# Splitting every weight of the first layer's front part, with the rests computed on GpSimd

## The chip, the cores and the metric

The kernel runs on one core of one Trainium2 chip, in one launch. The metric is the device time of the whole program in microseconds (us), and lower is better. A core has TensorE (PE, with its weight loads as PEld), VectorE (DVE), ScalarE (ACT), GpSimd (POOL) and SyncE (SP), which here issues all the transfers, and 16 DMA engines that carry them out.

## The reference

The reference is a decoder trunk with two layers over 256 tokens of 2048 channels, all in float32. Cut to what matters here:

```python
c_act = silu(c)
for l in range(2):
    mod = c_act @ w_mod[l] + b_mod[l]                  # w_mod[l]: 2048 x 12288
    shift1, scale1, gate1, shift2, scale2, gate2 = split(mod, 6)
    h = rms_norm(x, norm1_gain[l]) * (1 + scale1) + shift1
    proj = h @ w_in[l]                                 # 2048 x 4884, for three mixers
    mix = concat(gla(proj), sliding_window(proj), gated_delta_net(proj))
    x = x + gate1 * (mix @ w_out[l])                   # 2048 x 2048
    h = rms_norm(x, norm2_gain[l]) * (1 + scale2) + shift2
    x = x + gate2 * ((silu(h @ w_gate[l]) * (h @ w_up[l])) @ w_down[l])   # 5632 wide
return rms_norm(x, final_norm_gain)
```

## The kernel before, in words

**Streamed products.** Every large product goes through `stream`. The activations (two blocks of 128 tokens, transposed) are the stationary operand, and the weights move through TensorE. A job is one step of 128 rows of a weight by up to 1024 columns, loaded by one or two transfers into a buffer `raw` (L321), and used for both blocks of tokens; its columns go to two banks of 512. There are two ways to take a job:

- Split: ACT writes a rounded copy `wh` of the weights (L328), another engine writes the exact rest `wl` = `raw` - `wh` (L329, on VectorE before), and TensorE makes three passes: high by high, high by low, low by high. `raw`, `wh` and `wl` have three buffers each.
- Whole: TensorE takes the float32 weights as they are. Nothing is split, so a job needs only one buffer, and whole jobs take turns in the nine buffers of `raw`, `wh` and `wl`. In the profile a whole job shows eight matmul records at up to 512 columns, for two blocks of tokens by two banks, and a split one twelve.

Where a `place` is given for a job, its split weights stay in `hm` buffers instead (L335 on ACT, L336 on VectorE), so that the first block of tokens can run ahead of the second. `tail` gives places to the last jobs of a product.

**The front of layer 0** is what comes before its first FFN. It has four stages. First the input projection for the gated DeltaNet and the sliding window (groups `qk`, `z`, `v`, `bq`; 1024, 520, 768 and 1024 columns) runs in four blocks of K, each of four steps of 128 rows, so 16 jobs a block and 64 in all. A block of K can start when the shift and scale of its channels are there. Then come the DeltaNet and the sliding window, together with two more projections for the linear attention (16 jobs of 1024 and 16 of 528 columns). Then the output projection: 24 jobs over channels 512 to 2047, during which the linear attention runs, and a last 8 jobs over the first 512 channels. At last the second norm. Before the change, `WHOLE_IN[0]` takes all 64 jobs of the first stage whole, `WHOLE_A[0]` three of the second and `WHOLE_OUT[0]` all 32 of the third; the other 29 jobs are split.

**The modulation** `c_act @ w_mod` is computed on VectorE: a step loads a piece of `w_mod` and adds its weighted rows to sums (`scalar_tensor_tensor`, L221, with two inputs in SBUF). The first four segments of shift and scale come in 128 early steps of 512 columns, in scratch buffers `g`; the others in steps of 1024 columns in two buffers `mraw`. `tick` puts steps between the jobs at a rate that `RATE_IN`, `RATE_A` and `RATE_OUT` set; a segment's sums are cleared on POOL (L210) and finished by TensorE transposes into `fin` (L246). When the second norm comes, the gate of the mixer and the second shift and scale must be complete.

**Order.** A scheduler orders the instructions of each engine when the program is built, by the order in which the code names them and by when it expects them to be ready; on the chip each engine, and SP's queue of transfers, then runs its list in order. Tiles of a tag are handed out in turn, and an instruction or transfer waits until the earlier user of its buffer is done.

**Other names.** `mix` holds the transposed outputs of the mixers; `to_mix` and `split_mix` split them into two `hm` tiles each where the output projection takes split operands. `norm` writes `hm` pairs too (L459 on ACT, L460 on VectorE). `hm` has 28 buffers. The whole second layer, and the FFNs of both, use split jobs with the rest on VectorE.

Of the kernel before, what the change touches and what calls it, by code (L numbers as in the profile page):

```python
# [10 lines left out]
F32 = mybir.dt.float32  # L11
# [5 lines left out]
ALU = mybir.AluOpType  # L17
AX = mybir.AxisListType

P = 128  # L20
# [14 lines left out]
# The first layer's input projection runs in blocks of K, each as soon as its shift and  # L35
# scale are known; sizes in chunks of 128.
# [6 lines left out]
WHOLE_IN = (True, False)  # L43
WHOLE_A = (3, 0)
RATE_LAST = 1.6
WHOLE_OUT = ((0, 1, 2, 3), ())
XN_ACT = ((False, False), (False, False))
# Steps of the modulation per 1024-column step of the other products, by layer.
# [10 lines left out]
# Columns of w_in.  # L59
# [3 lines left out]
def _constants():  # L63
    """Shape-only constants, [P, n]: name -> (offset, width), and the array."""
    i = np.arange(P)
    row, col = i[:, None], i[None, :]
    freq = (ROPE_THETA ** (-np.arange(8) / 8.0)).astype(np.float32)
    parts = {
        "ident": row == col,
        "upper": col >= row,  # L70
        "lower": row > col,
        "freq": np.tile(freq[None], (P, 1)),
    }
    for m in LEVELS:
        sib = ((row // m) ^ 1) == (col // m)
        parts[f"up{m}"] = sib & (col > row)
        if m > 1:
            parts[f"lo{m}"] = sib & (row > col)
    keys = np.arange(2 * P)[None, :]
    dist = row + P - keys  # L80
    parts["band"] = np.where((dist >= 0) & (dist < P), 0.0, NEG)
    parts = {n: a.astype(np.float32) for n, a in parts.items()}
    where, at = {}, 0
    for n, a in parts.items():
        where[n] = (at, a.shape[1])
        at += a.shape[1]
    return where, np.ascontiguousarray(np.concatenate(list(parts.values()), 1))
# [5 lines left out]
# Small per-layer parameters, [P, n].  # L93
# [10 lines left out]
def trunk(ctx: ExitStack, tc, x, cT, pos, small, consts, b_mod, w_mod, w_in, w_gk, w_out,  # L104
# [25 lines left out]
    # Small products run in two banks of their own, and the third serves the sliding-window  # L130
    # and linear attention, or the others while those rest.
# [10 lines left out]
    def bc(ap, n, axis):  # L142
        """Insert a broadcast axis of n at `axis`."""
        ap = ap.unsqueeze(axis)
        shape = list(ap.shape)
        shape[axis] = n
        return ap.to_broadcast(shape)

# [50 lines left out]
    def mod_segment(l, part, k0, nk):  # L199
        """Steps that leave channels k0*128.. of `part` in mod_col or gate_row."""  # L200
# [60 lines left out]
    # Steps are traced a few at a time between those of the other products, and a segment's  # L261
    # end some steps later, when its sums are there. The rows of a gate have room for one
    # gate: the next one's steps wait for the last use of this one.
    # While `hold` has a value, the next step waits for it: a norm's short operations, on
    # which all else waits, are not to queue behind steps that have time.
# [25 lines left out]
    def stream(groups, ks, lhs, whole=(), lead=(), tail=()):  # L291
        """groups: (segs, evac); segs: (dram [K, n], column, width) whose widths fit 1024
        together, each one bank. lhs(k, blk, whole) -> stationary, high and low or whole.
        evac(blk, j, psum) when a product is complete.
        whole: the steps that take float32 operands as they are, in one product that costs
        TensorE four passes: for times when VectorE is busier.
        lead, tail: where the split weights of the first and last steps stay while the first
        block of rows runs ahead of the second (None: among the others)."""
# [12 lines left out]
        def load(job, n, place):  # L311
# [13 lines left out]
            if place is None:  # L325
                wh = tl(wsp, [P, 1024], "wh", F32R)
                wl = tl(wsp, [P, 1024], "wl", F32R)
                A.activation(wh[:, :width], raw[:, :width], AF.Copy)  # L328
                V.tensor_tensor(wl[:, :width], raw[:, :width], wh[:, :width].bitcast(F32),  # L329
                                ALU.subtract)  # L330
                return [(wh[:, o:o + s[2]], wl[:, o:o + s[2]]) for s, o in zip(segs, offs)]
# [52 lines left out]
    def split(src, scale=None):  # L384
        """Rounded part and exact rest of a [P, 512] value, scaled per partition if asked."""
        h = tl(hmp, [P, 4, P], "hm", F32R)
        lo = tl(hmp, [P, 4, P], "hm", F32R)
        h2, lo2 = (t.rearrange("p a b -> p (a b)") for t in (h, lo))
        if scale is None:
            A.activation(h2, src, AF.Copy)  # L390
            V.tensor_tensor(lo2, src, h2.bitcast(F32), ALU.subtract)
        else:
            A.activation(h2, src, AF.Copy, scale=scale)
            V.scalar_tensor_tensor(lo2, src, scale, h2.bitcast(F32), ALU.mult, ALU.subtract)
        return h, lo

    def transpose4(src, tag="mm"):
        """[P, 512] -> a bank of four transposed [P, P] blocks."""
# [5 lines left out]
    def rsqrt(pool, out, v):  # L404
        """out = v ** -0.5 for small [P, n] tiles, by Newton steps; v is used up."""
# [30 lines left out]
    def norm(l, sub, blk, r, res, ks=range(KD)):  # L436
        """Chunks `ks` of 128 channels into res[chunk // 4]: whole, high and low parts."""
# [69 lines left out]
    def gated(l, pool, tag, o_ap, zg, blk, group, gain, scale=None, tag_ps="mm"):  # L507
        """o_ap: [P, 4 heads, 128], to be scaled per head by `scale` first."""
# [29 lines left out]
    def gdn(l, pool, pc, zg, cbca):  # L538
        """pc[group][blk]: q, k, v token-major before the convolution."""
# [25 lines left out]
        for blk in range(NB):  # L565
# [10 lines left out]
            # log1p(e) = 2 atanh(s), s = e / (2 + e) <= 1/3  # L576
# [41 lines left out]
        # v / |k|, token-major  # L618
# [130 lines left out]
    def gla(l, pool, qk_tok, v_tok, zg, lr):  # L749
        """qk_tok[blk]: [P, 512] q then k of four heads of 64; lr[blk]: [P, 16]."""  # L750
# [102 lines left out]
    def rope(pool, ap, blk, heads):  # L853
        """ap: [P, heads, >= 16], rotated in place on its first 16 columns."""
# [10 lines left out]
    def swa_keys(pool, kv):  # L865
        """kv[blk]: [P, 256], k of two heads then v of two heads."""
# [14 lines left out]
    def swa(l, pool, blk, g, q_tok, kT, kv):  # L881
        """Eight heads of key-value head g for one block of queries; q_tok: [P, 512]."""
# [70 lines left out]
    def layer(l):  # L953
        wi, wo = w_in[l], w_out[l]
        load_small(l)
# [10 lines left out]
        def land(first, last, pieces, after=None):  # L966
            """Evacuation of products whose K is cut: pieces(blk, j) -> (dst, lo, hi, func)."""
# [63 lines left out]
        if len(blocks) > 1:  # L1031
            # A tag's tiles are given out in order: these before those that turn over.
# [89 lines left out]
        as_.close()  # L1122

# [98 lines left out]
```

## Time and profile before

| | |
|---|---|
| time, median of three runs | 2594.43 us (2592.87 to 2595.39) |
| profiled execution, span from first to last instruction | 2596.9 us; the page lists no other time for it |
| busy: PE, PEld | 2450.9 us (94%), 1900.8 us (73%) |
| busy: DVE, ACT, POOL | 1752.5 us (67%), 1068.2 us (41%), 26.3 us (1%) |
| moved by DMA | 600.79 MB, 231 GB/s over the span |
| layer 0 before its FFN | from the start to about 591 us |

Busy time counts an engine while an instruction of its own runs. A line of a timeline begins with the start of a group of instructions, its duration and its engine; "L356" is the line of the kernel, "x8" the number of instructions, and a bracket at the end the idle time in front, with who ended it. A table by stage gives, for each stretch of the span, the busy time and number of instructions of each engine, the granted TensorE clock, the share of the time that the DMA engines were busy, and GB/s. A row of waits names the engine and line that waited, for whom, the total, the number of waits and the longest.

### The profile page before, as it was taken

The numbers are of one execution on the slowest core, as the hardware profiler recorded it, in microseconds if no ns is written. First come the engines' busy times: TensorE is split into PE (matmuls) and PEld (weight loads), VectorE is DVE, ScalarE is ACT, GpSimd is POOL, SyncE is SP. The second block draws the span as 40 slices with busy tenths as digits, with TensorE's granted clock in tenths as the row PEclk, the third lists the DMA queues.
The fourth block names the chain that finished last, engine by engine and source line by source line (L and its number), as shares of the span: only waits on it lengthen the run. The fifth ranks groups of instructions, "written<-read, shape, count | busy, mean of one in ns | idle before, by whom it ended". The sixth has DMA issues, their size and how long they took to land.

```text
span 2596.9 us, 31018 instructions
## 1 busy us (share of the span) xinstructions
PE 2450.9 (94%) x11164; PEld 1900.8 (73%) x11164; DVE 1752.5 (67%) x2527; ACT 1068.2 (41%) x1582; POOL 26.3 (1%) x72
## 2 busy tenths in 40 slices
PE   3999999979999999999998999999899999999997
PEld 2555785547788777788877788877678878888876
DVE  6767876776666777657678788678674575544555
ACT  2203444124444333444345454654544434344443
POOL 0000000000000000000000000000000000000000
PEclk9999999989999999999999999999999999999999
DMA  9996548767778888868687865356576686666654
GB/s 329 373 317 210 179 133 271 263 214 264 262 261 266 288 281 277 288 194 305 219 274 244 280 209 157 94 176 208 204 258 192 199 281 194 188 193 189 186 179 154
DMA packets 190034, 600.79 MB, mean 231 GB/s; under 512 B 21628, under 2 KB 26268, under 8 KB 189496
## 3 DMA queue, kind: packets, MB, share of 16 engines
q1 hardware_dynamic: 189880, 598.81, 70.6%
q8 instruction: 87, 1.43, 0.2%
q14 instruction: 67, 0.55, 0.1%
HBM read 596.63 MB, written 2.10 MB: 231 GB/s over the span
## 4 chain that ended last, share of the span: by engine, by line
PE 57%; DMA 21%; DVE 12%; issue 6%; ACT 3%; SPq 0%; POOL 0%; DVEq 0%; ACTq 0%; POOLq 0%
PE acc L356 49%; DMA mraw<-in_w_mod 13%; DVE wl L329 4%; DVE acc L221 3%; DMA raw<-in_w_down 3%; DMA raw<-in_w_up 2%; DMA raw<-in_w_gate 1%; DMA raw<-in_w_in 1%; PE ga L830 1%; ACT wh L328 1%; PE mm L401 1%; PE ga L401 1%; PE ga L897 1%; DVE g L221 1%; PE mm L688 1%
## 5 line engine op out<-in xcount | busy, mean ns | idle before, releaser
L356 PE MATMUL acc<-wh,hm 128*128 128x512 f32 (+3 forms) x4872 | 1346.7, 390 | 23.3 <-ACT acc L425 5.3
L328 ACT ACTIVATE wh<-raw 128x1024 fp32r<-128x1024 f32 (+3 forms) x669 | 684.7, 1026 | 993.1 <-PE acc L356 592.1
L329 DVE TENSOR_TENSOR wl<-raw,wh 128x1024 fp32r<-128x1024 f32 (+3 forms) x669 | 785.1, 1179 | 451.0 <-ACT wh L328 449.6
L356 PEld LDWEIGHTS acc<-wh,hm 128*128 128x128 f32 x4872 | 896.1, 190 | 216.6 <-issue 17.0
L356 PE MATMUL acc<-wl,hm 128*128 128x512 f32 (+3 forms) x2484 | 795.2, 394 | 9.9 <-DVE wl L329 7.4
L221 DVE SCALAR_TENSOR_TENSOR acc<-mraw,c_act,acc 128x1024 f32<-128x1024 f32 x320 | 410.3, 1282 | 214.5 <-DMA mraw<-in_w_mod 212.5
L356 PEld LDWEIGHTS acc<-wl,hm 128*128 128x128 f32 x2484 | 458.5, 190 | 116.7 <-DVE wl L329 16.7
L356 PE MATMUL acc<-wh,ahl 128*128 128x512 f32 x560 | 157.9, 396 | 0.0
L356 PEld LDWEIGHTS acc<-wh,ahl 128*128 128x128 f32 x560 | 105.6, 189 | 24.5
L221 DVE SCALAR_TENSOR_TENSOR g<-g,c_act,g 128x512 f32<-128x512 f32 x128 | 88.8, 745 | 13.4 <-DMA g<-in_w_mod 13.4
L356 PE MATMUL acc<-wl,ahl 128*128 128x512 f32 x280 | 90.8, 398 | 4.6 <-DVE wl L329 4.4
L356 PE MATMUL acc<-wh,b 128*128 128x512 f32 (+2 forms) x184 | 75.0, 547 | 3.2 <-ACT b L456 2.1
L356 PE MATMUL acc<-raw,b 128*128 128x512 f32 (+2 forms) x176 | 66.8, 518 | 0.8 <-DVE g L973 0.7
L356 PE MATMUL acc<-wl,b 128*128 128x512 f32 (+2 forms) x176 | 66.1, 513 | 1.3 <-DVE g L973 1.3
L356 PEld LDWEIGHTS acc<-wl,ahl 128*128 128x128 f32 x280 | 52.5, 189 | 19.2 <-DVE wl L329 7.2
L356 PEld LDWEIGHTS acc<-wh,b 128*128 128x128 f32 x184 | 35.3, 198 | 33.3 <-issue 23.9
L456 ACT ACTIVATE b<-mm,mod,mod 128x128 f32<-128x128 f32 x24 | 9.2, 462 | 111.5 <-DVE mod L254 94.0
L356 PEld LDWEIGHTS acc<-wl,b 128*128 128x128 f32 x176 | 32.6, 190 | 28.6 <-issue 21.3
L356 PEld LDWEIGHTS acc<-raw,b 128*128 128x128 f32 x176 | 32.6, 190 | 27.4 <-issue 22.0
L933 DVE TENSOR_TENSOR acc<-acc,gate 128x512 f32<-128x512 f32 x64 | 43.2, 693 | 9.0 <-PE acc L356 8.9
L935 DVE TENSOR_TENSOR xs<-xs,acc 128x512 f32<-128x512 f32 x64 | 42.2, 678 | 0.1
L356 PE MATMUL acc<-raw,hm 128*128 128x512 f32 x88 | 41.8, 597 | 0.0
(320 smaller groups left out, 1662.7 us busy)
## 6 DMA issues: line engine op xcount, KB each, us to landing
mraw<-in_w_mod SPq DMA_DIRECT2D x320, 512.0 KB
raw<-in_w_down SPq DMA_DIRECT2D x176, 512.0 KB
raw<-in_w_gate SPq DMA_DIRECT2D x160, 512.0 KB
raw<-in_w_up SPq DMA_DIRECT2D x160, 512.0 KB
raw<-in_w_in SPq DMA_DIRECT2D x72, 512.0 KB
g<-in_w_mod SPq DMA_DIRECT2D x128, 256.0 KB
raw<-in_w_out SPq DMA_DIRECT2D x43, 512.0 KB
raw<-in_w_in SPq DMA_DIRECT2D x32, 264.0 KB
```

Source lines behind the costliest of these rows:

```text
L221: V.scalar_tensor_tensor(acc, raw[:, a], c_act[:, i + a:i + a + 1], acc, ALU.mult, ALU.add)
L328: A.activation(wh[:, :width], raw[:, :width], AF.Copy)
L329: V.tensor_tensor(wl[:, :width], raw[:, :width], wh[:, :width].bitcast(F32), ALU.subtract)
L356: TE.matmul(ps[blk, j][:, :segs[j][2]], xa, parts[j][part], start=i == 0 and n == 0, stop=last and n == len(terms) - 1)
L401: TE.transpose(ps[:, j * P:(j + 1) * P], src[:, j * P:(j + 1) * P], ident)
L456: A.activation(h32[:, i], ps[:, i * P:(i + 1) * P], AF.Identity, scale=mod_col[l, 3 * sub + 1, at + i], bias=mod_col[l, 3 * sub, at + i])
L688: TE.matmul(ps[:, s], LT[blk][:, s], Tm[blk][:, s], start=True, stop=True)
L830: TE.matmul(p4[:, g, blk], lhs_t[rows, g, s], rhs_t[rows, g, s], start=True, stop=True)
L897: TE.matmul(ps[:, j * nk:(j + 1) * nk], qT[rows, i + j], kT[rows, g, :nk], start=True, stop=True)
L933: V.tensor_tensor(ps, ps, need(gate_row, (l, part, j)), ALU.mult)
L935: V.tensor_tensor(x_j, x_j, ps, ALU.add)
```

## The change

The three settings `WHOLE_IN`, `WHOLE_A` and `WHOLE_OUT` of layer 0 become empty, so every job of the first layer's front is split. A list `rest` names the engine that computes the rest `wl`: GpSimd in layer 0 up to the end of the output projection, VectorE from then on. The split that puts its results into places (L336) still names VectorE. As `WHOLE_OUT[0]` is empty, `to_mix` and `split_mix` now split the mixers' outputs in layer 0 as they do in layer 1, and the last 8 jobs of the output projection take `ahead(*TAIL_OUT)` as layer 1 does: two of them in `wh` and `wl`, six in `hm` places, and all eight run for the first block of tokens before the second. Comments are left out of the new file, too, which changes no instruction.

```diff
-WHOLE_IN = (True, False)
-WHOLE_A = (3, 0)
+WHOLE_IN = (False, False)
+WHOLE_A = (0, 0)
 RATE_LAST = 1.6
-WHOLE_OUT = ((0, 1, 2, 3), ())
+WHOLE_OUT = ((), ())
...
+    rest = [V]
...
                 A.activation(wh[:, :width], raw[:, :width], AF.Copy)
-                V.tensor_tensor(wl[:, :width], raw[:, :width], wh[:, :width].bitcast(F32),
-                                ALU.subtract)
+                rest.append(rest.pop(0))
+                rest[0].tensor_tensor(wl[:, :width], raw[:, :width],
+                                      wh[:, :width].bitcast(F32), ALU.subtract)
                 return [(wh[:, o:o + s[2]], wl[:, o:o + s[2]]) for s, o in zip(segs, offs)]
...
     def layer(l):
         wi, wo = w_in[l], w_out[l]
+        rest[:] = [G] if l == 0 else [V]
...
         as_.close()
+        rest[:] = [V]
```

## The prediction

> **What bounds the kernel now.** I read the page first, then the busy times by stage, then what TensorE waited for in the stage that the change rewrites.
>
> ```profile
> span 2596.9 us, 31018 instructions
> PE 2450.9 (94%) x11164; PEld 1900.8 (73%) x11164; DVE 1752.5 (67%) x2527; ACT 1068.2 (41%) x1582; POOL 26.3 (1%) x72
> ```
>
> TensorE is busy nearly throughout and POOL is idle, so work for POOL looks free. The change touches only the time before the first FFN, so I cut that into its stages.
>
> ```profile
> core 0: us, PE busy (x) PEld busy (x) DVE busy (x) ACT busy (x) POOL busy (x), PEclk, DMA share, GB/s
> 42.00:88.00 46.00, 45.62 (x136) 25.48 (x137) 30.67 (x48) 9.95 (x24) 1.05 (x2) 1.00 1.01 369
> 88.00:140.00 52.00, 51.22 (x163) 27.96 (x161) 43.73 (x75) 10.39 (x24) 1.45 (x14) 1.00 1.02 371
> 140.00:187.00 47.00, 46.85 (x142) 25.70 (x142) 26.28 (x42) 2.27 (x6) 0.00 (x0) 1.00 0.87 307
> 187.00:222.00 35.00, 32.29 (x96) 17.36 (x94) 24.93 (x73) 6.73 (x15) 0.00 (x0) 1.00 0.85 279
> 222.00:404.00 182.00, 175.65 (x1034) 139.00 (x1034) 145.19 (x350) 85.01 (x196) 1.91 (x2) 0.96 0.52 164
> 404.00:534.00 130.00, 120.45 (x438) 62.37 (x438) 89.16 (x148) 32.16 (x67) 2.86 (x3) 1.00 0.82 273
> 534.00:591.00 57.00, 47.04 (x142) 26.27 (x143) 43.11 (x77) 25.27 (x62) 0.95 (x1) 0.88 0.52 168
> 591.00:2597.00 2006.00, 1928.45 (x9008) 1574.54 (x9006) 1320.31 (x1643) 885.13 (x1166) 13.45 (x26) 0.99 0.70 225
> ```
>
> The first four rows are the four K blocks of the input projection (the last up to where the DeltaNet starts), then the mixers, the 24 jobs of the output projection, and its last 8 with the norm. In the first two blocks TensorE and the DMA engines are both full: no gain on TensorE can shorten them. In the third and fourth TensorE leads. In the output projection the chain of waits shows a third party:
>
> ```profile
> PE acc L356 <- ACT b L456: 2.1, 1, 2.1
> PE acc L356 <- DVE g L973: 2.0, 3, 1.1
> by line: DMA mraw<-in_w_mod 32.1%; PE acc L356 24.5%; DVE acc L221 12.3%; PE ga L830 8.8%; DMA wh<-in_w_out 3.6%; ACT s L456 3.1%; issue 2.8%; ACT hm L459 1.7%; DVE a L524 1.2%; DVE xs L935 1.0%; ACT a L512 0.8%; DVE acc L933 0.8%; PE fin L
> 410.87 1.28 DVE acc L221
> 412.17 5.91 DMA mraw<-in_w_mod
> SPq L218 <- DVE acc L221: 54.8, 30, 6.8
> ```
>
> The first two rows are nearly all that TensorE waited for from 42 to 222 us: whole products keep it fed. The next three are from the chain of waits between 404 and 590 us: loads and steps of the modulation hold 32.1% and 12.3% of it, TensorE's products 24.5%, and the two single rows show how: a step ends, its buffer's next load takes 5.91 us, the next step follows. The last says that between 404 and 534 us SP waited 54.8 us for those buffers. That stage is set by the modulation's two buffers as much as by TensorE.
>
> **The change part by part.** *TensorE.* A whole job of 1024 columns starts 3.43 us after the one in front (95.83 to 99.26). A split job makes 12 passes; in the FFN, where TensorE was busy without a gap, 298 matmuls took 65 us, 0.218 us each, so 2.6 us.
>
> ```profile
> 95.83 3.60 PE L356 MATMUL acc<-raw,b 128*128 128x512 f32 x8
> 99.26 3.60 PE L356 MATMUL acc<-wh,b 128*128 128x512 f32 x8
> 1105.00:1170.00 65.00, 65.00 (x298) 53.83 (x297) 35.51 (x34) 28.15 (x30) 0.96 (x1) 1.00 0.67 197
> ```
>
> I take a quarter, 0.86 us a job and less where it is narrower: a K block has 3336 columns by 4, 13.0 such jobs, so 11.2 us a block and 45 us in all four, 2.6 us for the three jobs of the linear attention, 27.5 us for the 32 jobs of the output projection: 75 us of TensorE time.
>
> *ACT* gets 99 more copies of 1.06 us. A block's are 13.0 by 1.06, 14 us beside the 9.95 busy of 46: hidden, though each job now has ACT and the rest in front of it. `wh` and `wl` have three buffers, about 7.8 us of TensorE's work, for a chain of some 3.5 us, so I cost it at nothing; the loads keep their number and their place in SP's queue. But whole jobs had nine buffers, 31 us of work ahead; now three raw and three split ones hold 15 us, and SP's longest wait for a modulation buffer, 6.8 us above, fits into that. If it does not, what is late next is `raw`.
>
> ```profile
> L221 DVE SCALAR_TENSOR_TENSOR acc<-mraw,c_act,acc 128x1024 f32<-128x1024 f32 x320 | 410.3, 1282 | 214.5 <-DMA mraw<-in_w_mod 212.5
> L221 DVE SCALAR_TENSOR_TENSOR g<-g,c_act,g 128x512 f32<-128x512 f32 x128 | 88.8, 745 | 13.4 <-DMA g<-in_w_mod 13.4
> L328 ACT ACTIVATE wh<-raw 128x1024 fp32r<-128x1024 f32 x605 | 640.9, 1061 | 933.2 <-PE acc L356 568.2 <-DMA raw<-in_w_down 116.0 <-DMA raw<-in_w_up 105.0
> L329 DVE TENSOR_TENSOR wl<-raw,wh 128x1024 fp32r<-128x1024 f32 x605 | 736.4, 1222 | 436.0 <-ACT wh L328 435.4
> L460 DVE TENSOR_TENSOR hm<-s,hm 128x512 fp32r<-128x512 f32 x16 | 11.1, 691 | 13.5 <-ACT hm L459 13.5
> L450 DVE TENSOR_SCALAR s<-xs,rms 128x512 f32<-128x512 f32 x16 | 7.7, 479 | 0.0
> L210 POOL MEMSET acc<- 128x1024 f32 x20 | 19.0, 954 | 1644.6 <-PE fin L246 1146.2 <-DVE mraw L233 479.7 <-ACT neg L912 18.8
> L210 POOL MEMSET g<- 128x512 f32 x8 | 4.2, 526 | 104.1 <-DMA g<-in_consts 36.8 <-DMA g<-in_w_mod 35.0 <-DVE g L221 30.0
> L216 POOL COPY mraw<-hm 128x1 f32<-128x1 f32 x2 | 1.4, 719 | 67.3 <-ACT hm L459 67.3
> ```
>
> *The rest on POOL.* No row shows POOL with two inputs. Its memsets give a stream's price: (954 - 526) / 512, 0.84 ns a column. The only one that reads, a copy of one column, takes 0.72 us. At the low end one stream and no start, 0.95 us for 1024 columns; at the high end two reads and a write one after the other with the start, 3.3 us; I take two streams and the start, 2.4 us (1.6 at 520 columns, 2.0 at 768), nearest to the copy that reads. A block then holds 33.8 us of POOL (12.8 to 45), beside TensorE's 34. Of 128 jobs, 122 go there: six in the tail keep L336 on VectorE. The Trainium skill, "GPSIMD Engine Reference", section "Elementwise — side-by-side cycle accounting", gives 4497 ns for a two-input operation of 2048 columns; half of it, 2.25 us, is an estimate from that page, and with it the sum below would be about +25 us. No run here shows it.
>
> *Beside VectorE.* The price that decides is whether POOL's two reads and VectorE's two-input steps run at the same time. The trace cannot show it: POOL hardly reads. Its bounds are full overlap and full exclusion. One hint is in the rows: at 512 columns VectorE takes 0.48 us with one tensor input and 0.69 us with two, so the second input does cost a read path. I take exclusion for two-input steps. The modulation's steps are the bulk of those:
>
> ```profile
> 42.00:88.00 46.00, 26.39 (x38) 1.00 1.01 369
> 88.00:140.00 52.00, 30.54 (x44) 1.00 1.02 371
> 140.00:187.00 47.00, 16.46 (x19) 1.00 0.87 307
> 187.00:222.00 35.00, 14.30 (x12) 1.00 0.85 279
> 222.00:404.00 182.00, 38.38 (x30) 0.96 0.52 164
> 222.00:404.00 182.00, 27.04 (x29) 0.96 0.52 164
> 404.00:534.00 130.00, 48.68 (x38) 1.00 0.82 273
> ```
>
> All are L221 but the sixth, which is the 29 rests of L329 that leave VectorE. With 1.4 us of L460 a block, POOL and two-input steps in turn need 26.4 + 33.8 + 1.4 = 61.6 us in the first block (+15.6), 65.7 in the second (+13.7), 51.7 in the third (+4.7); in the fourth, 12 jobs (24.1 us) with 14.3 and 1.4 make 39.8 (+4.8): +38.8 us when the DeltaNet starts. With overlap the first two gain nothing (DMA is full), the third at most 8 us (307 GB/s for 47 us is 38.9 us at 371), the fourth TensorE's 7.7: -15.7 us.
>
> The Trainium skill says in "SBUF — State Buffer", section "Who interferes with whom", that a VectorE instruction with two SBUF inputs and a GpSimd instruction that reads SBUF block each other, the second until the first has ended. By that rule the exclusion is full and the sum stands as I make it; without it the sum would be that of the first rival. It speaks against the change, and no run here shows it yet.
>
> *Mixers, 222 to 404 us.* POOL's 74 us there and the steps' 38.4 fit into 182; TensorE, busy 175.65, saves 6 us (four `bq` jobs, three others), and 27 us leave VectorE. With exclusion some rests come late: 0; with overlap -6.
>
> *Output projection.* TensorE's 24 jobs save 20.6 us, but the modulation holds the stage. POOL 58 us, L221's 48.7 and 5.5 us for eight splits of `mix` (0.69 each) make 113; with all of VectorE's work 89.2 + 5.5 + 58 = 153: -4 (TensorE's gaps) to +23, I take +10, since each step that waits for POOL delays its buffer's load. With overlap -5. The splits find their `hm` buffers free only as the projections end, so the first job waits for one rest of 0.69 us and the copy in front of it, which lies inside the +10. In the tail the first block of tokens ends earlier and its norm can begin under the second, but twelve L336 halves of 0.69 us come onto VectorE: -3 (-7 to +8).
>
> *POOL's queue.* The L210 memsets wait for `fin` (rows above); nothing was behind them, now rests are. Six before the FFN, up to 2.4 us each: inside the range, 0 in the sum.
>
> The sum is 38.8 + 0 + 10 - 3, +46 us. It stands on the profiled span of 2596.9 us, 2.5 us above the median; the difference goes onto the median: 2640 us.
>
> **The rivals.** *No exclusion, faster.* If VectorE's steps run beside POOL unhindered, the terms are -15.7 - 6 - 5 - 3, -30 us: 2565 us. For it speaks that POOL is idle and VectorE loses 27 us; against it the two-input price. Between the two, a share of 30 / (30 + 46), 0.39 of the full exclusion, is where it turns. *POOL is itself too slow:* at 3.3 us a block holds 45 us, above TensorE; the blocks then add 80 us, the output projection about 23, less 3: 2694 us. *The lost lead:* the raw buffers fall behind in SP's queue; 30 waits of 54.8 us show, and a quarter of them uncovered is +14: 2608 us. *A wash:* a share near 0.39, 2594 us. That rests stay on VectorE in the tail makes the change less than its name, in six jobs.
>
> **How the numbers follow.** A measurement here can tell about 0.2%, 5.2 us. With the share even over 0 to 1, 0.39 lies on the fast side and 0.61 on the slow; POOL's unknown price moves some to either. Chances: the forecast 0.45, no exclusion 0.30, POOL too slow 0.12, a wash 0.08, the lost lead 0.05. So faster 0.30, same 0.08, slower 0.62. The likeliest case alone spans 2610 to 2670 us. The range runs from 2560, beyond the overlap end, to 2685, and leaves most of the too-slow case out.
>
> **What would show it.** After the change, TensorE's waits from 42 to 222 us should name POOL's `wl`; L221's mean should rise above 745 and 1282 ns, or gaps appear in front of it; POOL's spacing should be 2.4 us or more; the DeltaNet should start near 260 us and the FFN near 637. If L221 keeps its mean, POOL's spacing stays under 2.6 us and the DeltaNet starts near 206, the exclusion is wrong, and with it the sign.

## The result and the profile after

The changed kernel takes 2697.51 us (2695.55 to 2704.24, four runs), against 2594.48 for the kernel before: 1.0395 times as long, 95% interval 1.0376 to 1.0415. That is 103 us more, where 46 were forecast; the time lies 12.5 us above the range. All ratios below are to the kernel before; where a difference in microseconds stands beside one, it is the ratio less one times 2594.5.

First the top of the page after the change, then the busy times in the first three stretches that the prediction used, with those of the mixers and of the output projection as they now lie.

```profile
span 2694.3 us, 32254 instructions
PE 2456.5 (91%) x11560; PEld 1987.6 (74%) x11560; DVE 1870.4 (69%) x2518; ACT 1158.1 (43%) x1689; POOL 305.8 (11%) x194
```

```profile
42.00:88.00 46.00, 34.23 (x155) 27.55 (x156) 43.65 (x40) 18.75 (x36) 28.70 (x15) 0.91 0.86 292
88.00:140.00 52.00, 40.68 (x174) 31.11 (x174) 45.66 (x54) 17.16 (x27) 28.84 (x15) 0.88 0.78 262
140.00:187.00 47.00, 33.52 (x135) 24.77 (x136) 45.78 (x46) 15.76 (x23) 29.17 (x12) 0.91 0.82 288
264.00:461.00 197.00, 170.65 (x1041) 142.04 (x1041) 159.48 (x321) 93.35 (x205) 77.14 (x38) 0.96 0.53 168
461.00:687.00 226.00, 176.97 (x726) 132.09 (x725) 175.61 (x247) 87.34 (x166) 69.95 (x31) 0.82 0.59 195
```

TensorE and DMA, both full in the first two blocks before, are now both short of work: 34.23 of 46 us and a DMA share of 0.86. VectorE is busy for 43.65 of 46, 45.66 of 52 and 45.78 of 47, and has become the bound there. Over the whole run its total went from 1752.5 to 1870.4 us, though 29 rests left it. The groups of instructions up to 700 us show which of its instructions became longer, and what one costs on POOL (columns: busy, mean ns of one, idle time in front):

```profile
L221 DVE SCALAR_TENSOR_TENSOR acc<-mraw,c_act,acc 128x1024 f32<-128x1024 f32 x100 | 154.6, 1546 | 39.1 <-DMA mraw<-in_w_mod 38.8
L221 DVE SCALAR_TENSOR_TENSOR g<-g,c_act,g 128x512 f32<-128x512 f32 x128 | 131.5, 1085 | 2.9 <-DMA g<-in_w_mod 2.9
L818 DVE TENSOR_TENSOR a<-a,a 128x256 f32<-128x256 f32 x16 | 11.6, 762 | 1.4 <-ACT a L813 1.4
L454 DVE TENSOR_SCALAR b<-xs,rms 128x512 f32<-128x512 f32 x8 | 7.6, 945 | 0.0
L521 DVE TENSOR_SCALAR gss<-gss 128x4 f32<-128x4 f32 x4 | 4.8, 1210 | 0.0
L978 DVE TENSOR_TENSOR g<-g,acc 128x512 f32<-128x512 f32 x18 | 11.8, 678 | 1.8 <-PE acc L360 1.7
L694 DVE TENSOR_TENSOR g<-mm,masks 128x512 f32<-128x512 f32 x12 | 8.3, 689 | 4.1 <-PE mm L692 3.9
L333 POOL TENSOR_TENSOR wl<-raw,wh 128x1024 fp32r<-128x1024 f32 x74 | 195.4, 2651 | 195.3 <-ACT wh L331 187.8 <-DMA raw<-in_w_in 5.3 <-DMA raw<-in_w_out 2.1
```

The modulation's steps went from 1281 to 1546 ns and from 745 to 1085. L818 went from 414 to 762 ns. L521, four columns wide with one tensor input, went from 168 to 1210, of which one instruction of the four took 3.26 us. L978 and L694, which take one of their two inputs from PSUM, stayed at 678 and 689 (682 and 687 before). L818 and L521 were these lines before:

```profile
L814 DVE TENSOR_TENSOR a<-a,a 128x256 f32<-128x256 f32 x16 | 6.1, 414 | 0.3 <-ACT a L809 0.2
L517 DVE TENSOR_SCALAR gss<-gss 128x4 f32<-128x4 f32 x4 | 0.7, 168 | 4.5 <-ACT a L512 4.5
```

The timeline shows single cases in the second block (start, length):

```profile
96.99 2.36 POOL L333 TENSOR_TENSOR wl<-raw,wh 128x1024 fp32r<-128x1024 f32 x1 [5.06 <-ACT wh L331]
97.42 1.96 DVE L254 SCALAR_TENSOR_TENSOR mod<-sums,gains 128x4 f32<-128x4 f32 x1
99.96 0.47 DVE L454 TENSOR_SCALAR b<-xs,rms 128x512 f32<-128x512 f32 x1
102.60 2.66 POOL L333 TENSOR_TENSOR wl<-raw,wh 128x1024 fp32r<-128x1024 f32 x1 [3.25 <-ACT wh L331]
102.94 2.60 DVE L454 TENSOR_SCALAR b<-xs,rms 128x512 f32<-128x512 f32 x1
```

The rest starts at 96.99 and ends at 99.35; a VectorE instruction of four columns starts inside it and ends at 99.38. Without a rest beside it L454 takes 0.47 us; the next one starts 0.34 us after a rest and ends 0.28 us after it. VectorE waits inside its instruction until POOL's has ended, and everything in VectorE's order waits behind it.

The same holds for the modulation's steps, one by one. Of the 100 steps of 1024 columns up to 700 us, 58 overlap no rest; they take 1278 ns on the mean and 1286 at most. In 26 a rest has between 0.44 and 2.34 us to go when the step begins, and every one of them ends 1.08 or 1.09 us after that rest. In 12 a rest begins while the step runs; these keep 1.26 to 1.28 us, and the rest ends last. The other four begin in the last 0.07 us of a rest and take 1.27 or 1.28 us.

Of each run the times follow, of e4 the time alone, because its profiled execution, at 3077.32 us and a granted clock of 0.749, was a slow one, which its ratio leaves out. The marks of the stages: the DeltaNet's first transposes, the mixers' last 264-column product, and POOL's copy in L216 as the FFN starts. Between the first two marks TensorE runs some 1030 matmuls in the kernel before and some 1040 to 1060 in the changed kernel, e10, e13, e14 and e15, so they enclose nearly the same work. The marks are those of one execution: e2's took 2585.76 us, where the median of its ten is 2605.43.

| kernel | ratio (95% interval) | us | DeltaNet | end of mixers | FFN |
|---|---|---|---|---|---|
| before | 1 | 0 | 225 | 404 | 591 |
| after | 1.0395 (1.0376 to 1.0415) | +102 | 264 | 461 | 687 |
| e1 all rests on VectorE | 1.0197 (1.0158 to 1.0236) | +51 | 232 | 425 | 644 |
| e2 POOL writes, raw read early | 1.0026 (1.0001 to 1.0051) | +7 | 222 | 390 | 580 |
| e7 POOL writes, raw read late | 1.0038 (1.0018 to 1.0058) | +10 | 224 | 397 | 602 |
| e10 the same behind ACT's copy | 1.0021 (1.0002 to 1.0039) | +5 | 223 | 390 | 593 |
| e8 POOL copies raw twice | 1.0146 (1.0114 to 1.0178) | +38 | 241 | 421 | 623 |
| e3 whole jobs, three buffers | 1.0106 (1.0080 to 1.0132) | +28 | 239 | 411 | 612 |
| e4 input projection alone | 1.0279 (1.0247 to 1.0312) | +72 | | | |
| e5 output projection alone, and rests of before, on POOL | 1.0208 (1.0181 to 1.0234) | +54 | 223 | 416 | 637 |
| e6 the 29 rests of before on POOL | 1.0067 (1.0038 to 1.0095) | +17 | 224 | 416 | 599 |
| e11 output projection alone, VectorE | 1.0106 (1.0079 to 1.0134) | +28 | 224 | 400 | 615 |
| e12 its last 8 jobs alone, VectorE | 0.9992 (0.9978 to 1.0005) | -2 | 224 | 396 | 589 |
| e9 the third K block alone, VectorE | 0.9985 (0.9967 to 1.0004) | -4 | 223 | 391 | 584 |
| e13 reads in the first stage only | 1.0131 (1.0099 to 1.0162) | +34 | 263 | 431 | 623 |
| e14 reads in the mixers only | 1.0174 (1.0135 to 1.0214) | +45 | 228 | 432 | 634 |
| e15 reads in the output projection only | 1.0121 (1.0090 to 1.0152) | +31 | 223 | 391 | 615 |
| e16 third block and last 8 jobs, VectorE | 1.0001 (0.9985 to 1.0017) | 0 | 223 | 394 | 585 |

From the FFN's start to the end the two profiled executions differ by 2 us (2007.6 and 2005.9): nearly the whole loss lies ahead of it.

### The profile page after: what moved, and what is told of

The parts are those of the page before. It is cut to its first block, busy times and chain, and to the rows that moved or that the text cites. A ratio compares the mean times of both kernels' runs of the same rounds, so it can differ in the third digit from the quotient of the medians.

```text
span 2694.3 us, 32254 instructions
## 1 busy us (share of the span) xinstructions
PE 2456.5 (91%) x11560; PEld 1987.6 (74%) x11560; DVE 1870.4 (69%) x2518; ACT 1158.1 (43%) x1689; POOL 305.8 (11%) x194
## 4 chain that ended last, share of the span: by engine, by line
PE 52%; DMA 20%; DVE 14%; issue 7%; ACT 3%; POOL 2%; SPq 1%; DVEq 0%; ACTq 0%; POOLq 0%
PE acc L360 45%; DMA mraw<-in_w_mod 10%; DVE wl L333 4%; DVE acc L221 4%; DMA raw<-in_w_down 3%; DMA raw<-in_w_in 3%; POOL wl L333 2%; DMA raw<-in_w_up 2%; PE ga L834 1%; DVE g L221 1%; ACT wh L331 1%; DMA raw<-in_w_gate 1%; DMA g<-in_w_mod 1%; PE mm L405 1%; PE ga L405 1%
## 5 line engine op out<-in xcount | busy, mean ns | idle before, releaser
L360 PE MATMUL acc<-wh,hm 128*128 128x512 f32 (+3 forms) x5536 | 1533.6, 389 | 47.9 <-ACT wh L331 15.7
L331 ACT ACTIVATE wh<-raw 128x1024 fp32r<-128x1024 f32 (+3 forms) x762 | 772.8, 1016 | 1162.2 <-PE acc L360 626.2
L360 PEld LDWEIGHTS acc<-wh,hm 128*128 128x128 f32 x5536 | 1025.7, 192 | 262.1 <-ACT wh L331 31.1
L360 PE MATMUL acc<-wl,hm 128*128 128x512 f32 (+2 forms) x2768 | 884.3, 390 | 38.7 <-POOL wl L333 27.5
L360 PEld LDWEIGHTS acc<-wl,hm 128*128 128x128 f32 x2768 | 517.5, 193 | 153.9 <-POOL wl L333 40.2
L221 DVE SCALAR_TENSOR_TENSOR acc<-mraw,c_act,acc 128x1024 f32<-128x1024 f32 x320 | 436.8, 1365 | 199.1 <-DMA mraw<-in_w_mod 196.7
L333 POOL TENSOR_TENSOR wl<-raw,wh 128x1024 fp32r<-128x1024 f32 (+3 forms) x122 | 279.7, 2304 | 289.5 <-ACT wh L331 278.4
L221 DVE SCALAR_TENSOR_TENSOR g<-g,c_act,g 128x512 f32<-128x512 f32 x128 | 131.5, 1085 | 2.9 <-DMA g<-in_w_mod 2.9
L834 PEld LDWEIGHTS ga<-a 64*128 64x128 f32 x224 | 32.5, 220 | 19.1 <-DVE a L841 9.2
L834 PE MATMUL ga<-a 64*128 64x128 f32 x224 | 38.4, 321 | 8.5 <-DVE a L841 6.2
L360 PE MATMUL acc<-hm,hm 128*128 128x512 f32 x144 | 38.0, 407 | 4.4 <-ACT hm L339 3.0
```

What stands on the lines that cost most here:

```text
L221: V.scalar_tensor_tensor(acc, raw[:, a], c_act[:, i + a:i + a + 1], acc, ALU.mult, ALU.add)
L333: rest[0].tensor_tensor(wl[:, :width], raw[:, :width], wh[:, :width].bitcast(F32), ALU.subtract)
L360: TE.matmul(ps[blk, j][:, :segs[j][2]], xa, parts[j][part], start=i == 0 and n == 0, stop=last and n == len(terms) - 1)
L834: TE.matmul(p4[:, g, blk], lhs_t[rows, g, s], rhs_t[rows, g, s], start=True, stop=True)
```

## The experiments

The theory: POOL's reads of SBUF stop VectorE's steps (exclusion). The rivals: the order and the waits cost it (a rest on a queue of its own, behind ACT's copy; raw buffers held longer; fewer buffers in front), or the split itself does, wherever its rests are computed, or POOL is too slow by itself. The expectations call exclusion theory 1, the lead that is lost with fewer buffers theory 2, and the slow POOL theory 3.

**The rests back on VectorE (e1).**

```diff
-        rest[:] = [G] if l == 0 else [V]
+        rest[:] = [V]
```

> The changed kernel with all rests on VectorE again, three passes everywhere. Theory 1 (POOL's reads and VectorE's two-input steps shut each other out): nothing is left on POOL to shut out, VectorE gets 122 rests of 0.7 to 1.22 us, which fit into its gaps except in the second K block (43.7 + 12.5 of 52 us): 2575 to 2605 us, L221 back at 1.28 and 0.745 us. Theory 2 (the lead: split jobs have three raw buffers where whole ones had nine, and their loads queue behind the modulation's): the buffers stay as in the changed kernel, so the time stays near 2697, 2670 to 2700 us. Theory 3 (POOL is too slow by itself at 2.4 us a job, with no exclusion): as theory 1, 2575 to 2605 us.

It takes 51 us more than before, half of the loss, and lies between the ranges of the theories. So the split by itself does not pay here either: it puts 99 more jobs' rests on VectorE. But POOL makes the same rests cost another 51 us, although it takes them off VectorE.

**POOL's time without its reads (e2, e7, e10).** Each rest on POOL is replaced by memsets and one-column copies. The rests are left out. Shown is e10.

```diff
-                rest[0].tensor_tensor(wl[:, :width], raw[:, :width],
-                                      wh[:, :width].bitcast(F32), ALU.subtract)
+                # e2: the column of raw first; e7: last; e10: last, and a column of wh first
+                if rest[0] is G:
+                    G.tensor_copy(wl[:, 0:1], wh[:, 0:1].bitcast(F32))
+                    G.memset(wl[:, 1:width - 1].bitcast(F32), 0.0)
+                    G.memset(wl[:, 1:width * 3 // 4].bitcast(F32), 0.0)
+                    G.tensor_copy(wl[:, width - 1:width], raw[:, 0:1])
...                                           # else the rest as before, on VectorE
```

> The changed kernel, but POOL computes no rests: in the place of each it copies one column of raw and writes two memsets, 0.72 + 0.95 + 0.74 us at 1024 columns, so it is busy as long as with a rest and hardly reads. The rests are left out of the result. Theory 1 (exclusion of reads): L221 falls back to 1.28 and 0.745 us, the DeltaNet starts at 205 to 225 us and the time is 2560 to 2600 us. Theory 2 (lead): the raw buffers are held as before or a little shorter, 2670 to 2700 us. Theory 3 (POOL too slow by itself): POOL is as busy, 2670 to 2700 us.

> As the run with writes in the place of the rests, but the one column of raw is read after the two memsets, so raw stays held as long as POOL works on the job; the rests are left out of the result. It separates the lead from the exclusion. Theory 1 (exclusion): as the run before, 2580 to 2615 us. Theory 2 (lead: raw buffers held through ACT and POOL): most of the loss is back, 2640 to 2690 us.

> The changed kernel, but in place of each rest POOL first copies one column of wh (so it waits for ACT's copy, as the rest does), then fills wl by two memsets, and copies one column of raw last (so it holds raw as long). The rests are left out; order, waits and POOL's length stay near the rest's, only the streaming reads are gone. Exclusion by reads: near the run of the writes alone with the late read of raw, 2600 to 2615 us, DeltaNet at 222 to 228, L221 at 1282 and 745 ns. Cost of the order (the rest behind ACT on a queue of its own, raw held longer): 2640 to 2690, DeltaNet at 240 or later with L221 at 1282.

e2 gave 7 us more than before, e7 10, e10 5, all within about 1 us of the ranges for exclusion. In e10 POOL waits for ACT as the rest does, holds raw until its end, and is busy almost as long: 268.9 us against 305.8 (about 2.4 us a job at 1024 columns: 366, 950, 745 and 311 ns). Only the streaming reads are gone, and 97 of the 102 us with them. Here are the engines on e10's page, and then its steps of the modulation up to 700 us:

```profile
PE 2425.3 (93%) x11560; PEld 1965.1 (76%) x11560; DVE 1752.9 (67%) x2518; ACT 1159.5 (45%) x1691; POOL 268.9 (10%) x560
```

```profile
L221 DVE SCALAR_TENSOR_TENSOR acc<-mraw,c_act,acc 128x1024 f32<-128x1024 f32 x117 | 149.8, 1280 | 51.0 <-DMA mraw<-in_w_mod 50.4
L221 DVE SCALAR_TENSOR_TENSOR g<-g,c_act,g 128x512 f32<-128x512 f32 x128 | 89.0, 747 | 21.4 <-DMA g<-in_w_mod 21.3
```

The same groups in e2:

```profile
L221 DVE SCALAR_TENSOR_TENSOR acc<-mraw,c_act,acc 128x1024 f32<-128x1024 f32 x120 | 153.7, 1281 | 56.9 <-DMA mraw<-in_w_mod 56.2
L221 DVE SCALAR_TENSOR_TENSOR g<-g,c_act,g 128x512 f32<-128x512 f32 x128 | 89.2, 748 | 23.2 <-DMA g<-in_w_mod 21.8 <-issue 0.8 <-DVE hm L469 0.3
```

VectorE runs 2518 instructions in the changed kernel and 2518 in e10, in 1870.4 and 1752.9 us: 117.5 us that its instructions took longer, against 97 of time. The steps are back at 1280 and 747 ns. All that e10 keeps of the change, the order, the waits, the lead and TensorE's saving, comes to 5 us net (interval 0.5 to 10).

**One read instead of two (e8).** POOL copies raw whole into `wl` twice; the rests are left out.

```diff
-                rest[0].tensor_tensor(wl[:, :width], raw[:, :width],
-                                      wh[:, :width].bitcast(F32), ALU.subtract)
+                if rest[0] is G:
+                    G.tensor_copy(wl[:, :width], raw[:, :width])
+                    G.tensor_copy(wl[:, :width], raw[:, :width])
...                                           # else the rest as before, on VectorE
```

> POOL copies the whole of raw twice into wl in the place of each rest: one tensor read at a time, about as long in all; the rests are left out of the result. If any read by POOL keeps VectorE's second read out, L221's mean rises to 1.4 to 1.6 us (1024) as in the changed kernel and the time is 2640 to 2700 us. If only POOL's two-input operations do, L221 stays at 1.28 us and the time at 2580 to 2615 us.

```profile
L221 DVE SCALAR_TENSOR_TENSOR acc<-mraw,c_act,acc 128x1024 f32<-128x1024 f32 x113 | 158.4, 1403 | 41.6 <-DMA mraw<-in_w_mod 41.3
L221 DVE SCALAR_TENSOR_TENSOR g<-g,c_act,g 128x512 f32<-128x512 f32 x128 | 118.4, 979 | 7.7 <-DMA g<-in_w_mod 7.6
```

Two instructions of 1218 and 1290 ns at 1024 columns, each with one input, hold the steps at 1403 and 979 ns. So one read is enough to hold them. It cost 38 us, which is 8 below the range expected for it and less than the rest's 102; whether that is the shorter single read or the start ahead of ACT's copy was not told apart.

**The lead alone (e3).** The kernel before, its whole jobs in the three raw buffers only.

```diff
-                pool, tag = ((rawp, "raw"), (wsp, "wh"), (wsp, "wl"))[which[1] % 3]
+                pool, tag = rawp, "raw"
```

> The kernel before, but whole jobs use only the three raw buffers where they took turns in nine. Nothing is split that was not. Theory 2 (lead): the loads fall behind as in the changed kernel and most of the 103 us appears, 2650 to 2700 us. Theories 1 and 3 (POOL): the kernel has no POOL work, three whole jobs are 10 us of lead, and it stays within 2590 to 2615 us.

It cost 28 us, between the ranges of the theories and twice what the rival of the lost lead had. A whole job holds its buffer until TensorE has used it, a split one only until its rest is made, so I take this as a bound and not as the split's own price.

**One part of the change at a time (e4, e5, e6).** e4 splits the input projection only, e5 the output projection only (both with POOL's rests), e6 nothing more than before, with its 29 rests moved to POOL. The edits are of the changed kernel.

```diff
 # e4
-WHOLE_OUT = ((), ())
+WHOLE_OUT = ((0, 1, 2, 3), ())
 # e5
-WHOLE_IN = (False, False)
+WHOLE_IN = (True, False)
 # e6: both; in all three
-WHOLE_A = (0, 0)
+WHOLE_A = (3, 0)
```

> Only the input projection is split with rests on POOL; the three jobs of the linear attention and the whole output projection are as in the kernel before (the 29 other rests of the mixers' stage stay on POOL). All theories that hold per stage: the DeltaNet starts near 264 us as in the changed kernel (+39), and the output projection takes its 187 us as before, so 2594 + 39 + 0 to 18 for the mixers: 2633 to 2655 us. If the output projection's part of the loss (+39 us) came only from a shift that began in the first stage, the time would be 2680 or more.

> The other part alone: the output projection split with rests on POOL (and the 29 rests of the mixers' stage on POOL), the input projection and three jobs of the linear attention whole as before. If the stages' losses add, the 103 us of the change less the 73 us of the input projection alone leave +30: 2620 to 2640 us. If the output projection's loss came only from what the first stage pushed in front of it, 2590 to 2605 us.

> The kernel before with only its 29 rests of the mixers' stage moved from VectorE to POOL; all whole jobs stay whole. Theory 1 (exclusion): VectorE loses 27 us of its own and is kept out for up to POOL's 64 us beside it, where TensorE is busy 175 of 182 us: 2592 to 2612 us. Theory 3 (POOL slow, no exclusion): VectorE was at 145 of 182 us and gets free, 2575 to 2597 us. L221 in 222 to 404 us should rise above 1.28 us under theory 1 alone.

e4 gave 72 us, e5 54, e6 17. The 29 rests are in both of the first two, so 72 + 54 - 17 = 109 stands against 102: the parts add up within their intervals, of 7 to 8 us each way. By their ratios e4 and e5 take 2667 and 2648 us, each above its expected range. e6 is the clearest refutation of a term: nothing is split there that was not split before, 27 us of rests leave VectorE, and the kernel is 17 us slower, with L221 at 1337 ns up to 700 us where 1281 stood.

**The output projection on VectorE (e11), and its tail (e12).**

```diff
 # of before; e11
-WHOLE_OUT = ((0, 1, 2, 3), ())
+WHOLE_OUT = ((), ())
 # e12
-WHOLE_OUT = ((0, 1, 2, 3), ())
+WHOLE_OUT = ((1, 2, 3), ())
```

> The kernel before with only the output projection split, all rests on VectorE. If what the output projection lost is POOL's reads: FFN at 591 to 598, 2594 to 2602 us. If the splitting itself costs it there (28 us of rests and 5.5 of splits of mix on VectorE beside the modulation's steps, fewer buffers in front, the twelve half rests of the tail): 20 to 32 us more, FFN at 611 to 623, 2615 to 2627, with L221 at its old means.

> The kernel before with only the last 8 jobs of the output projection split (the first three groups of K stay whole), rests on VectorE, tail kept for the second block of tokens. If the loss of the output projection lies in its tail and the norm: 10 to 20 us more than before, 2605 to 2615. If it lies in the 24 jobs in front: within 5 us of before, or up to 5 faster, because TensorE saves 6.9 us there and the first block's norm begins earlier: 2589 to 2599.

e12 gave -2 us, so the tail with its twelve half rests and the norm cost nothing that can be measured, net of what TensorE saves there. e11 gave +28 with no rest on POOL at all. Below are the output projection's busy times in the kernel before, in e11, and in e10, and what SP waited for there in e11:

```profile
404.00:591.00 187.00, 167.49 (x580) 88.64 (x581) 132.27 (x224) 57.43 (x129) 3.81 (x4) 0.96 0.73 241
```

```profile
400.00:615.00 215.00, 168.57 (x707) 129.20 (x708) 170.29 (x267) 89.96 (x167) 3.85 (x4) 0.83 0.65 212
```

```profile
390.00:593.00 203.00, 173.84 (x727) 129.72 (x725) 145.41 (x246) 89.81 (x169) 58.51 (x104) 0.84 0.67 221
```

```profile
SPq L218 <- DVE acc L221: 84.3, 36, 9.0
SPq L321 <- DVE wl L329: 25.6, 16, 4.4
```

VectorE has 170.29 us of 215, against 132.27 of 187, and SP stands 84.3 and 25.6 us waiting for steps and rests (63.6 and 10.6 before). Not all of the 28 us need be VectorE's: TensorE is busy as long as before, though a quarter of its work in these jobs was to go, and its granted clock is 0.83 where 0.96 stood. In e11 eight matmuls of L830 take 1.16 us at 456.62 and 2.07 at 462.81; what lowers the clock isn't shown. e10, with the same split and a clock of 0.84, has 25 us less on VectorE there and a stage 12 us shorter.

**In which stage the reads cost (e13, e14, e15).** e10 with the real rests in one stage only; elsewhere they are left out and replaced as in e10.

```diff
+    stage = [1, 1]         # e13; e14: [1, 2], e15: [1, 3]
...
-                if rest[0] is G:
+                if rest[0] is G and stage[0] != stage[1]:
...
+                stage[0] = 2      # ahead of the DeltaNet; 3 ahead of the output projection
```

> The changed kernel with the real rests on POOL in the first stage only (up to the DeltaNet, about 86 of 122); the later rests are left out and replaced by the short copies and memsets that wait and last like them. If the price of POOL's reads belongs to the stage in which they are made: about 39 us over the run without streaming reads, 2635 to 2645 us, DeltaNet at 260 to 266, later stages as without reads. If a late modulation carries the loss on into the later stages: 2655 or more.

> The changed kernel with the real rests on POOL only for the 36 jobs between the DeltaNet's start and the output projection; the others are left out and replaced as before. If the mixers' loss is made in that stage by the reads: 13 to 20 us over the run without reads, 2612 to 2622 us. If it was carried over from the first stage: 2600 to 2606.

> The changed kernel with the real rests on POOL only for the 26 jobs of the output projection; the earlier ones are left out and replaced as before. If the output projection's loss is made there by the reads: 25 to 38 us over the run without reads, 2625 to 2640 us, FFN 215 us or more after the last product of the mixers. If the prediction's +7 was right for the stage by itself and the rest was carried over: 2604 to 2612.

Less the 5 of e10, the reads cost 28 us in the first stage (60 rests there, not the 86 of the expectation), 40 in the mixers (36) and 26 in the output projection (26), each give or take some 10. Their sum, 94, stands against 97 for all: they add up. e13 lies below its expected range and e14 far above its own. The marks say the same stage by stage. Against e10, the first stage is 40 us longer in e13, the mixers 36 in e14, and the output projection 22 in e15; no stage behind the reads is longer by more than 1 us, so no stage's loss is the echo of another's. The steps up to 700 us, first in e13 and then in e15:

```profile
L221 DVE SCALAR_TENSOR_TENSOR acc<-mraw,c_act,acc 128x1024 f32<-128x1024 f32 x113 | 150.2, 1329 | 70.7 <-DMA mraw<-in_w_mod 70.3
L221 DVE SCALAR_TENSOR_TENSOR g<-g,c_act,g 128x512 f32<-128x512 f32 x128 | 136.4, 1122 | 4.0 <-DMA g<-in_w_mod 4.0
```

```profile
L221 DVE SCALAR_TENSOR_TENSOR acc<-mraw,c_act,acc 128x1024 f32<-128x1024 f32 x113 | 159.0, 1407 | 45.9 <-DMA mraw<-in_w_mod 40.6 <-DMA raw<-in_w_in 4.6
L221 DVE SCALAR_TENSOR_TENSOR g<-g,c_act,g 128x512 f32<-128x512 f32 x128 | 89.3, 746 | 21.4 <-DMA g<-in_w_mod 21.3
```

Only where the reads are do the steps get longer: the 512-column ones of the first stage in e13, the 1024-column ones of the output projection in e15. In e13 the output projection is 11 us shorter than in e10; why isn't shown. In e14 6 of the 41 us lie ahead of the DeltaNet's mark, where two of its 36 rests already run. The mixers of e10, and then of e14:

```profile
222.00:390.00 168.00, 161.86 (x1041) 136.45 (x1041) 128.49 (x326) 93.04 (x204) 72.73 (x147) 0.99 0.58 190
```

```profile
228.00:432.00 204.00, 178.10 (x1058) 147.40 (x1058) 165.15 (x328) 92.37 (x206) 71.96 (x42) 0.93 0.50 159
```

VectorE is busy 37 us longer there with two instructions more. The modulation's steps are 10 us of that (51.93 for 34, against 42.20 for 33); the rest is in other instructions, such as one of four columns in L626 that takes 2.30 us where its twin takes 0.15.

**A faster version (e9, e16).** The two places where TensorE's saving might come through without POOL: the third K block (e9), and that with the last 8 jobs of the output projection (e16, the edit of e12 added).

```diff
-            gemm(segs, ks, lhs, land(first, last, at), whole=ks if WHOLE_IN[l] else (),
+            gemm(segs, ks, lhs, land(first, last, at), whole=ks if WHOLE_IN[l] and bi != 2 else (),
```

> The kernel before with only the third K block of the input projection split, rests on VectorE, no POOL. There TensorE leads (46.85 us busy of 47) and DMA has 13% to give: with the rests hidden, up to 8 us less, 2586 to 2590 us. If the rests on VectorE hold up the modulation's steps or the fewer buffers in front cost as much, 2594 to 2604.

> The kernel before with the third K block and the last 8 jobs of the output projection split, rests on VectorE, nothing on POOL: the two parts that cost nothing by themselves. If TensorE's savings there (up to 7.7 and 6.9 us) come through: 2584 to 2592 us. If the modulation holds the end of both stages anyway: 2592 to 2598.

e9 gave -4 us (interval -9 to +1), e16 0 (-4 to +4). e9 lies just above its faster range, e16 in the range for a modulation that holds the end of both stages. No version beat the kernel before by more than can be told from no change.

## Why the prediction was off

**The mechanism was right.** It took full exclusion of VectorE's steps by POOL's reads, and named the sign by that. Four of its signs came: the steps' means rose above 745 and 1282 ns, TensorE's waits from 42 to 222 us name POOL's `wl` first, a rest takes 2.36 us alone and 2651 ns on the mean where 2.4 was taken, and the DeltaNet starts at 264 us where 260 was named. The fifth failed: the FFN starts at 687 and not at 637.

```profile
PE acc L360 <- POOL wl L333: 12.3, 14, 2.2
SPq L218 <- DVE g L221: 46.4, 41, 4.6
SPq L324 <- POOL wl L333: 42.6, 21, 6.0
```

These are waits of TensorE and SP from 42 to 222 us in the changed kernel. TensorE's own wait for POOL is the small one; SP's 46.4 us (27.2 before) for the modulation's steps and 42.6 for POOL show where the time goes: loads start late.

The Trainium skill, "SBUF — State Buffer", section "Who interferes with whom", had the rule on which the sum stood. The runs agree: 1281 to 1546 and 745 to 1085 ns beside POOL's reads, 1280 and 747 beside its writes alone in e10, and no change where one input comes from PSUM (682 to 678). The same section counts VectorE's `tensor_scalar` among the operations that can take the shared ports, which the prediction left out: L454 with its one tensor input went from 479 to 945 ns.

**The first stage, +38.8: measured +39.** POOL's time and the steps' in turn made the stage's length, block by block: the first rests of the four blocks of K and the first one behind them start at 40.5, 109.7, 170.0, 219.9 and 259.9 us, so the blocks last 69, 60, 50 and 40 us, where 61.6, 65.7, 51.7 and 39.8 were worked out. The first rest runs before TensorE can start, at 46. VectorE is busy, waiting included, for 43.65, 45.66 and 45.78 us of the first three stretches. In e10 the DeltaNet starts at 223, so against it the reads make 41.

**The mixers, 0: the step that failed.** The prediction set POOL's 74 us and the steps' 38.4 against 182 and found room. The measured stage is 18 us longer in the changed kernel, the 29 rests of before cost 17 by themselves (e6), and the reads of the mixers' 36 rests make the stage 36 us longer (e14 against e10). Room in the sum of busy times is not cover. The work there is in order on VectorE (145.19 of 182 us busy before), TensorE's products and the modulation wait behind each held instruction, and the exclusion reaches far past L221: of the 37 us by which VectorE's busy time grows in e14's mixers, L221 has 10. The prediction counted the modulation's steps alone as what could be held.

**The output projection with its norm, +10 - 3: measured +38.** The tail was right (e12: -2). The rest was mis-sized: the split with its 38 us more on VectorE costs 28 (e11), and the reads of 26 rests cost 26 us when POOL makes them (e15), one microsecond each. The prediction had put the 24 jobs at -4 to +23 and had chosen +10, though it had named the modulation as what holds the stage; by that reading every held step goes onto the end, and the upper end was the likelier one. Even that end is short of what was measured. (The prediction's sum of 58, 48.7 and 5.5 there is 112 and not 113; nothing hangs on it.) Here are the waits of SP in the 155 us from 461 to 616 after the change, where 54.8 us with 6.8 at the longest stood before in the 130 us from 404 to 534:

```profile
SPq L218 <- DVE acc L221: 96.2, 27, 23.4
SPq L324 <- POOL wl L333: 4.1, 2, 2.2
```

**The other rivals.** *No exclusion* had 2565 us. e10 shows the changed kernel with next to none: 2600 by its ratio, not faster than before. So the break-even share of 0.39 was wrong too; in these runs there is none. TensorE's 75 us bring nothing. The term was itself too large: up to the FFN TensorE is busy for 522.46 us before and for 496.31 in e10, 26 less, and in the output projection not less at all (167.49 before, 173.84 in e10, at granted clocks of 0.96 and 0.84). Where the saving went in the first stage is seen in e10's first block, and in the waits of TensorE and SP from 42 to 222 us:

```profile
42.00:88.00 46.00, 37.41 (x183) 29.05 (x181) 29.73 (x45) 19.42 (x35) 25.91 (x53) 1.00 0.89 313
```

```profile
PE acc L366 <- ACT wh L331: 16.5, 17, 3.5
SPq L324 <- ACT wh L331: 29.9, 24, 5.6
```

TensorE is busy for 37.41 of 46 us where it had 45.62, and waits 16.5 us for ACT's copies, of which whole jobs have none; SP waits 29.9 us for them with its next loads, and the rate of the transfers falls from 369 to 313 GB/s. I read that as a lead that is too short; e3, which takes away the lead alone, cost 28 us. So *the lost lead* is not a rival with 0.05 but, by this reading, a part of every case, and the statement that ACT's chain is covered at nothing failed. Whether the lead is all that eats the saving was not tried. *POOL too slow* named 2694 us, close to the time, by a cause that is not there: a rest takes 2.36 us alone and not 3.3. The Trainium skill's "GPSIMD Engine Reference", section "Elementwise — side-by-side cycle accounting", gave 2.25 us as an estimate, half of its 4497 ns at 2048 columns; the trace is nearer to the 2.4 that was taken.

In sum, the forecast was -30 without exclusion and 76 for exclusion; measured are +5 and 97. Both ends were off in the same direction.

## What to carry to other kernels

An idle GpSimd is no free engine beside a busy VectorE: price an offload by what its reads hold up there, and not by GpSimd's busy time; here each rest read by POOL cost 0.5 to 1.1 us of end time (28 / 60 to 40 / 36), and moving 29 of them off VectorE with nothing else changed cost 17 us. The test that separates reads from order and waits is cheap: put writes of the same length in place of the reads, behind the same waits. And before a saving on one engine is counted, ask what fed that engine: nine buffers of unsplit weights kept the transfers full in the first two blocks, and splitting them gave up that lead.

## What the runs showed of the hardware

A VectorE instruction of 128x4 elements can take microseconds beside a POOL read: the third line is such a one, 3.26 us in place of 0.17, in the changed kernel's timeline. It starts while the third of three rests runs, and ends at 581.80, as the memset behind them does (581.77). The mean of L412's four-column `grs` rose from 170 to 700 ns.

```profile
571.81 9.07 POOL L333 TENSOR_TENSOR wl<-raw,wh 128x1024 fp32r<-128x1024 f32 x3 [26.29 <-ACT wh L331]
576.07 2.55 DVE L221 SCALAR_TENSOR_TENSOR acc<-mraw,c_act,acc 128x1024 f32<-128x1024 f32 x1 [0.18 <-DMA mraw<-in_w_mod]
578.54 3.26 DVE L521 TENSOR_SCALAR gss<-gss 128x4 f32<-128x4 f32 x1
580.82 0.95 POOL L210 MEMSET acc<- 128x1024 f32 x1
```

The blocking goes both ways: the three rests in a row take 2.39, 3.38 and 3.38 us, where one alone takes 2.36, and the second begins while a step runs; the longest took 3718 ns. POOL's writes alone left the two-input steps as they were, but not the one-input TENSOR_SCALAR from SBUF to SBUF: L454's shape took 595 ns in e2, against 479.
